# Rotated chunks through ScalarE and a DMA, 512-column passes for paired chunks, and more dummy matmuls at the start

## The chip, the cores and the metric

The kernel runs on one core of one Trainium2 chip. The metric is device time in microseconds, the median of several executions. All times are of that one core; its engines are TensorE (PE, with its weight loads PEld), VectorE (DVE), ScalarE (ACT), GpSimd (POOL) and SyncE (SP), which issues nearly all DMAs.

## The reference

Two layers of a mixer over 256 tokens of width 1024, all in float32. Each layer normalises `x`, projects it to some 9600 columns, runs four causal attentions side by side (A: MoBA, which at 256 tokens is one causal block; B: a three-branch attention with compressed, selected and window keys; C: stick-breaking; D: three dilated window attentions, merged by their softmax denominators), gates each, projects each up to 1024 columns, merges the four with sigmoids, and adds an output projection to `x`. A last norm follows.

```python
def _rope(x, pos):                       # queries and keys of A and D, queries of B, some keys of B
    x1, x2 = x[..., :half], x[..., half:]
    return jnp.concatenate([x1 * cos - x2 * sin, x1 * sin + x2 * cos], axis=-1)
...
h = _rmsnorm(x, norm_w)
proj = jnp.einsum('bsd,dc->bsc', h, w_in)
...                                      # o_a, o_b, o_c, o_d: the four attentions
widened = jnp.stack([_merge_heads(o_a) * jax.nn.silu(ga), ...], axis=2)
u = jnp.einsum('bsiw,iwd->bsid', widened, w_up)
y = jnp.sum(merge_g * u, axis=2)
return x + y @ w_out
```

## The kernel before

**Products in three parts.** Every large product is made from 4-byte operands split into a high and a low half: the weight tile `raw` (512 KB, 128 x 1024) is loaded by SP, ScalarE casts it to the high half `wh` (`emit_hi`, line 327), VectorE subtracts to get the low half `wl` (`emit_lo`, line 335), which also frees `raw` for the next load (`emit_loads`, line 312). The activations are split the same way into `hh` and `hl`. TensorE adds `high x high`, `high x low` and `low x high`. There are 5 buffers for `raw` and 6 for each half. A "half" in the code is one such weight tile.

**Items.** `layer_items` (line 36) is the order of one layer: first `N2` (`av`, `cv`, the values of A and C, tokens as stationary operand, 256 columns of weights moving), then `T` items (weights stationary, the 256 tokens moving) for queries, keys and gates, `K` and `N` items for other values, `W1` for the small network of B, then 16 pairs of `M` (merge gate) and `U` (up projection), and last the output projection: `o0`, `o1` and the pair `o2`, `o3`, 256 columns each. A T item takes two weight tiles and 48 matmuls. `mm_N2` (line 521) picks its passes by which operands are ready; `mm_o0` (line 579) leaves the last quarter of `y` for the end.

**An order written ahead.** The program is built by a planner: `Clock` (line 57) estimates for each engine when it is free and for each tile when it is written, and the builder emits instructions in the order that this clock gives (`run_splits`, `fill`). On the chip each engine then follows its own list strictly in order, and so does SP's list of DMAs.

**PSUM.** Products go to a ring `pp` of 3 banks of 512 columns. What comes after an item is a generator in `POST` (line 1166); it returns the bank with `pp.put`.

**Rotated chunks.** For `aq`, `ak`, `bq` and the six `dq`, `dk` of a layer, `post_rope` (line 675) multiplies the bank by sines, 32 rows at a time and written 32 rows up or down, multiplies it by cosines, frees the bank, lets GpSimd add the two, and then, once a buffer is free, `stack` (line 661) splits the result for the scores:

```python
for r in range(4):
    i, o = slice(32 * r, 32 * r + 32), slice(32 * (r ^ 1), 32 * (r ^ 1) + 32)
    vec.tensor_tensor(out=t2[o], in0=b2[i], in1=sinF[i]..., op=ALU.mult)
vec.tensor_tensor(out=q..., in0=b2, in1=cosF..., op=ALU.mult)
pp.put(bank)
nc.gpsimd.tensor_tensor(out=q, in0=q, in1=t, op=ALU.add)
```

`q` is a buffer of the ring `qkv`, to which four slices of `xt` are lent while `x` is not needed; so these rows read `xt` in some chunks and `qkv` in others, and `t` is `rope`.

**Output.** `post_out` (line 1123) adds a 256-column bank to `x` and squares the new columns for the next norm; `out_done` (line 1245) starts the norm of a token tile `tt` (128 tokens) when its last chunk is done. In the next layer's first item, `norm_T` (line 484) transposes the normed tile on PE. Ahead of the last slot of `o2`/`o3` the tile `tt` = 0 is transposed (line 1330).

**Start.** Four dummy matmuls on a zero tile `warm` (line 1273), eight transposes that spread the norm weight, then the norm of `x` in pieces, its transposes, and the first projection.

Matmuls and vector operations are all recorded on line 151, in the wrapper that keeps the planner's clock; tiles tell them apart.

## Time and profile before

| | us |
|---|---|
| median of 3 executions | 634.83 (634.63 to 635.2) |
| the profiled execution | 634.86 |
| its span, first to last instruction | 632.9 |
| PE busy | 612.2 |
| DVE busy | 482.1 |
| ACT busy | 369.5 |
| POOL busy | 46.3 |

The profile is of one execution. A row "out<-in" names what an instruction writes and reads, with buffer numbers left out. Busy time of PE counts a matmul from its start to a modelled end, so matmuls that follow each other overlap; the distance of their starts is what a matmul costs in a row of them. Idle time carries the name of what ended it. Only idle time on the chain that sets the end costs anything.

### The profile page before, as it was taken

The page shows a single profiled execution, that of the slowest core. Times are in us where ns is not written, and L with a number is a line of the kernel's source. Part 1 is how long each engine was busy: PE and PEld are TensorE (multiplying, and loading weights), DVE is VectorE, ACT ScalarE, POOL GpSimd, SP SyncE. Part 2 cuts the span into 40 slices and gives each one's busy share as a digit, 9 for nine tenths or more (in the row PEclk, how much of TensorE's full clock was granted, in tenths as well). Part 3 has the DMA queues.
Part 4 walks back from the last instruction along what each step waited for, and adds up shares of the span by engine and source line. Part 5 has one row for each costly group of instructions (what it writes and reads, how often), then busy time and mean ns, then how long its engine had stood idle before and what let it go on. Part 6 is the DMA issues. An engine that isn't in the chain of part 4 may idle for free.

```text
span 632.9 us, 12881 instructions
## 1 busy us (share of the span) xinstructions
PE 612.2 (97%) x5192; PEld 587.3 (93%) x5192; DVE 482.1 (76%) x850; ACT 369.5 (58%) x657; POOL 46.3 (7%) x59
## 2 busy tenths in 40 slices
PE   7999999999999999999999999999989999999996
PEld 6999999999998999999999899889989989999995
DVE  5887788999976665677688678899999666566673
ACT  5636744655557888445474564543575678864452
POOL 3020100111200000000001101021110000000000
PEclk9999999999999999999999999999999999999998
DMA  8942456644444345677666155645437344466811
GB/s 282 335 147 79 155 192 243 238 162 148 142 161 153 127 140 168 214 246 237 210 211 227 43 192 167 234 168 208 158 100 223 112 166 150 136 205 193 291 62 67
DMA packets 34907, 112.22 MB, mean 177 GB/s; under 512 B 4256, under 2 KB 5280, under 8 KB 34848
## 3 DMA queue, kind: packets, MB, share of 16 engines
q1 hardware_dynamic: 34560, 111.07, 52.2%
q8 instruction: 41, 0.67, 0.4%
q0 software_dynamic: 144, 0.33, 0.3%
q14 instruction: 18, 0.15, 0.1%
q10 hardware_dynamic: 144, 0.00, 0.0%
HBM read 109.61 MB, written 2.10 MB: 177 GB/s over the span
## 4 chain that ended last, share of the span: by engine, by line
PE 64%; DVE 20%; ACT 7%; issue 6%; DMA 2%; POOL 1%; SPq 0%; POOLq 0%; ACTq 0%; DVEq 0%
PE pp L151 55%; DVE wl L151 8%; DVE rope L151 4%; PE psO L151 3%; PE psT L151 3%; ACT p L151 3%; PE psS L151 3%; ACT wh L151 2%; DVE xt L151 2%; DMA raw<-w_half_dram 2%; DVE hl L151 1%; DVE p L151 1%; DVE pd L151 1%; DVE qkv L151 1%; ACT hh L151 1%
## 5 line engine op out<-in xcount | busy, mean ns | idle before, releaser
L151 PE MATMUL pp<-hh,wh 128*128 128x256 f32 x1008 | 288.2, 286 | 2.2 <-DVE xt L151 1.8
L151 PE MATMUL pp<-hh,wl 128*128 128x256 f32 x1008 | 282.1, 280 | 4.5 <-DVE wl L151 4.4
L151 PE MATMUL pp<-hl,wh 128*128 128x256 f32 x1008 | 280.9, 279 | 0.0
L151 DVE TENSOR_TENSOR wl<-raw,wh 128x1024 fp32r<-128x1024 f32 (+2 forms) x198 | 233.1, 1196 | 48.0 <-ACT wh L151 47.2
L151 ACT CAST wh<-raw 128x1024 fp32r<-128x1024 f32 (+2 forms) x198 | 189.2, 979 | 53.7 <-DMA raw<-w_half_dram 24.3
L151 PEld LDWEIGHTS pp<-hh,wh 128*128 128x128 f32 x1008 | 189.4, 188 | 9.0 <-issue 5.5
L151 PEld LDWEIGHTS pp<-hh,wl 128*128 128x128 f32 x1008 | 189.5, 188 | 6.2 <-DVE wl L151 6.1
L151 PEld LDWEIGHTS pp<-hl,wh 128*128 128x128 f32 x1008 | 189.4, 188 | 0.1
L151 PE MATMUL pp<-wh,hh 128*128 128x256 f32 (+1 forms) x320 | 84.9, 285 | 1.0 <-ACT hh L151 1.0
L151 PE MATMUL pp<-wl,hh 128*128 128x256 f32 (+1 forms) x320 | 83.1, 279 | 1.3 <-DVE wl L151 1.2
L151 PE MATMUL pp<-wh,hl 128*128 128x256 f32 (+1 forms) x320 | 83.4, 281 | 0.0
L151 PEld LDWEIGHTS pp<-wh,hh 128*128 128x128 f32 x320 | 58.3, 192 | 2.5 <-ACT hh L151 1.7
L151 PEld LDWEIGHTS pp<-wl,hh 128*128 128x128 f32 x320 | 57.3, 188 | 1.9 <-DVE wl L151 1.9
L151 PEld LDWEIGHTS pp<-wh,hl 128*128 128x128 f32 x320 | 58.0, 191 | 0.0
L151 ACT ACTIVATE p<-p,small 128x128 f32<-128x128 f32 x96 | 40.0, 449 | 27.8 <-DVE small L151 27.1
L151 DVE TENSOR_TENSOR rope<-pp,sinF 32x512 f32<-32x512 f32 x72 | 49.5, 687 | 3.3 <-PE pp L151 1.4
L151 POOL TENSOR_TENSOR xt<-xt,rope 128x512 f32<-128x512 f32 x14 | 28.0, 1998 | 168.8 <-DVE xt L151 93.2
L151 PE MATMUL pp<-widl,wh 128*128 128x256 f32 x128 | 35.9, 281 | 1.1 <-DVE widl L151 1.1
L151 PE MATMUL pp<-widh,wh 128*128 128x256 f32 x128 | 36.0, 282 | 0.0
L151 PE MATMUL pp<-widh,wl 128*128 128x256 f32 x128 | 35.8, 279 | 0.0
L151 ACT ACTIVATE tm<-pp 128x512 f32<-128x512 f32 x32 | 18.9, 591 | 22.1 <-PE pp L151 22.1
L151 ACT COPY ptr<-psT 128x384 f32<-128x384 f32 x47 | 21.4, 478 | 17.6 <-PE psT L151 17.5
(142 smaller groups left out, 666.6 us busy)
## 6 DMA issues: line engine op xcount, KB each, us to landing
raw<-w_half_dram SPq DMA_DIRECT2D x178, 512.0 KB, 4.2
raw<-w_up_dram SPq DMA_DIRECT2D x32, 256.0 KB, 3.2
raw<-w_kvb_dram SPq DMA_DIRECT2D x4, 536.0 KB, 4.5
xt<-x_in_dram SPq DMA_DIRECT2D x4, 256.0 KB, 3.5
xt<-x_in_dram SPq DMA_DIRECT2D x2, 512.0 KB, 7.1
pd<-norm_w_dram SPq DMA_DIRECT2D x2, 512.0 KB, 5.6
x_mem<-xt SPq DMA_DIRECT2D x2, 512.0 KB, 5.4
xt<-x_mem SPq DMA_DIRECT2D x2, 512.0 KB, 6.0
```

The costliest lines, as they stand in the source:

```text
L151: return f(*a, **k)
```

## The change

- **Rotation.** `post_rope` copies the bank to SBUF on ScalarE and frees it. Four DMAs (`swap_rows`, 64 KB each) write the copy into `rope` with the 32-row groups exchanged. When the planner's clock says that they have landed, VectorE multiplies the exchanged tile by the sines and the copy by the cosines, 128 rows each, and adds the two. The sign table is stored in the other order. For `bq` the copy is also the unrotated query, as before.
- **Paired chunks.** `av`/`cv` and now also `o0`/`o1` and `o2`/`o3` are computed as 512 columns at once: a weight tile holds 2 of the 8 row blocks of both chunks, a bank holds one token tile of both. In the last layer's last token tile, `o2`/`o3` stay two banks of 256 columns. `o0`/`o1` do the first three weight tiles for both token tiles, then the fourth. `av`/`cv` are copied out in four pieces by ScalarE or VectorE (`post_copy2`). Planned positions follow.
- **Dummies.** 7 more dummy matmuls after the spread of the norm weight, 2 after the first transposes of the norm and 5 after the second. They are not entered in the planner's clock.

```diff
             it.append(("U", (i, c), 1))
-    it += [("N", "o0", 2), ("N", "o1", 2), ("N2", ("o2", "o3"), 4)]
...
         d = {"U": 1.3, "W1": 0.6}.get(kind, 2.6)
+        if kind == "N2":
+            pos += [p_ + 1.3 * j for j in range(n)]
+            p_ += 4 * d
+            continue
         for j in range(n):
             pos.append(p_)
-            if not (kind in ("N", "N2", "K") and j % 2 == 0):
-                p_ += d if kind not in ("N", "N2", "K") else 2 * d
+            if not (kind in ("N", "K") and j % 2 == 0):
+                p_ += d if kind not in ("N", "K") else 2 * d
...
+        left = [6] * 4
         count = [0, 0]
-        todo = [(tt, j, kk, p) for tt in range(2) for j in range(2) for kk in range(4) for p in range(3)]
+        todo = [(tt, j, p) for tt in range(2) for j in range(4) for p in range(3)]
...
             for i in range(2):
-                k = 2 * kk + i
-                c = count[j]
-                count[j] += 1
-                mm(banks[j][:, 256 * tt:256 * tt + 256], x[0][:, i, :], x[1][:, 256 * (k % 4):256 * (k % 4) + 256],
-                   start=(c == 0), stop=(c == 47))
-            h = 2 * j + kk // 2
-            left[h] -= 1
-            if not left[h]:
-                release(h0 + h)
+                c = count[tt]
+                count[tt] += 1
+                mm(banks[tt], x[0][:, i, :], x[1][:, 512 * i:512 * i + 512], start=(c == 0), stop=(c == 23))
+            left[j] -= 1
+            if not left[j]:
+                release(h0 + j)
             n += 1
-            if n % 3 == 0:
+            if n % 2 == 0:
                 yield
         yield
...
-    def mm_o0(banks, h0):
-
...
+    def mm_o(bank, tt, h0, j, c0, c1):
+
+        for i in range(2):
+            k = 2 * j + i
+            hi, lo = (w[h0 + j][:, 512 * i + c0:512 * i + c1] for w in (his, los))
+            a, b = (y[1][:, k, 128 * tt:128 * tt + 128] for y in (hh, hl))
+            o = bank[:, 0:c1 - c0]
+            mm(o, a, hi, start=(k == 0), stop=False)
+            mm(o, a, lo, start=False, stop=False)
+            mm(o, b, hi, start=False, stop=(k == KT - 1))
+            yield
...
+    def swap_rows(out_, in_):
+
+        for r in range(4):
+            dma(out=out_[32 * (r ^ 1):32 * (r ^ 1) + 32], in_=in_[32 * r:32 * r + 32])
+        clk.t["dma"] = max(clk.t["dma"], clk.idle(out_), clk.ready(in_)) + 0.7
+        clk.wr.setdefault(out_.name, {})[(0, 128, 0, 512)] = clk.t["dma"] + 2.0
+        clk.rd.setdefault(in_.name, {})[(0, 128, 0, 512)] = clk.t["dma"] + 2.0
+
     def post_rope(l, name, bank):
-        q, t = take(qkv), rope.get()
+        c, t = take(qkv), rope.get()
+        nc.scalar.copy(c, bank)
+        pp.put(bank)
+        swap_rows(t, c)
+        yield when(t)
+        q = c
         if name == "bq":
-            T_[l, "bqr"] = r = take(qkv)
-            nc.scalar.copy(r, bank)
-        b2 = bank.rearrange("p (a t) -> p a t", a=2)
-        t2 = t.rearrange("p (a t) -> p a t", a=2)
-        for r in range(4):
-            i, o = slice(32 * r, 32 * r + 32), slice(32 * (r ^ 1), 32 * (r ^ 1) + 32)
-            vec.tensor_tensor(out=t2[o], in0=b2[i], in1=sinF[i].unsqueeze(1).to_broadcast([32, 2, S]), op=ALU.mult)
-        vec.tensor_tensor(out=q.rearrange("p (a t) -> p a t", a=2), in0=b2,
-                          in1=cosF.unsqueeze(1).to_broadcast([128, 2, S]), op=ALU.mult)
-        pp.put(bank)
-        nc.gpsimd.tensor_tensor(out=q, in0=q, in1=t, op=ALU.add)
+            T_[l, "bqr"] = c
+            q = take(qkv)
+        v = lambda x: x.rearrange("p (a t) -> p a t", a=2)
+        rows = lambda x: x.unsqueeze(1).to_broadcast([128, 2, S])
+        vec.tensor_tensor(out=v(t), in0=v(t), in1=rows(sinF), op=ALU.mult)
+        vec.tensor_tensor(out=v(q), in0=v(c), in1=rows(cosF), op=ALU.mult)
+        vec.tensor_tensor(out=q, in0=q, in1=t, op=ALU.add)
         rope.put(t)
...
+    def post_copy2(l, names, banks):
+
+        for j, name in enumerate(names):
+            T_[l, name] = take(qkv)
+        for tt in range(2):
+            for j, name in enumerate(names):
+                copy_to(T_[l, name][:, 256 * tt:256 * tt + 256], banks[tt][:, 256 * j:256 * j + 256])
+            pp.put(banks[tt])
+        done.update((l, name) for name in names)
...
-    def post_out(l, c, tt, bank):
-        xs = xt[:, tt, 256 * c:256 * c + 256]
-        vec.scalar_tensor_tensor(out=xs, in0=bank[:, 0:256], scalar=0.25, in1=xs, op0=ALU.mult, op1=ALU.add)
+    def post_out(l, c, n, tt, bank):
+
+        c0, c1 = 256 * c, 256 * (c + n)
+        xs = xt[:, tt, c0:c1]
+        vec.scalar_tensor_tensor(out=xs, in0=bank[:, 0:c1 - c0], scalar=0.25, in1=xs, op0=ALU.mult, op1=ALU.add)
         pp.put(bank)
-        square(tt, 256 * c, 256 * c + 256, c)
...
-        if kind == "N2" and name[0] == "o2":
+        if kind == "N2" and name[0] == "o0":
+
+            banks = [pp.get(), pp.get()]
+            for js in ((0, 1, 2), (3,)):
+                for tt in range(2):
+                    for j in js:
+                        yield (lambda: mm_o(banks[tt], tt, h0, j, 0, 512),
+                               (lambda: out_done(l, 0, 2, tt, banks[tt])) if j == 3 else None, [h0 + j] if tt else [], j, tt)
+        elif kind == "N2" and name[0] == "o2":
             for tt in range(2):
-                for j in range(2):
+                last = l == L - 1 and tt
+                for c0, c1 in ((0, 256), (256, 512)) if last else ((0, 512),):
                     bank = pp.get()
-                    yield (lambda: mm_N(bank[:, 0:256], tt, h0 + 2 * j, 256, hh[1], hl[1]),
-                           lambda: out_done(l, 2 + j, tt, bank), [h0 + 2 * j, h0 + 2 * j + 1] if tt else [])
+                    for j in range(4):
+                        yield (lambda: mm_o(bank, tt, h0, j, c0, c1),
+                               (lambda: out_done(l, 2 + c0 // 256, (c1 - c0) // 256, tt, bank)) if j == 3 else None,
+                               [h0 + j] if tt and c1 == 512 else [], j, tt)
         elif kind == "N2":
             banks = [pp.get(), pp.get()]
-            yield (lambda: mm_N2(banks, h0, pend.pop(1), l),
-                   lambda: [add_post(post_copy(l, name[j], banks[j])) for j in range(2)], [])
...
+            yield (lambda: mm_N2(banks, h0, pend.pop(1), l), lambda: add_post(post_copy2(l, name, banks)), [])
...
-        p1.put(warm)
+        def keep_warm(n):
+            for _ in range(n):
+                tc.nc.tensor.matmul(psO[:, 0, 0:128], warm[:, 0:128], warm[:, 0:128], start=True, stop=True)
+
+        keep_warm(7)
...
         norm_T(0, 0, xs[0][0], 0)
+        keep_warm(2)
...
         norm_T(0, 1, xs[0][1], 0)
+        keep_warm(5)
+        p1.put(warm)
...
-                if kind == "N2" and name[0] == "o2" and si == 3 and l + 1 < L:
+            for si, (work, after, freed, *part) in enumerate(gen):
+
+                if kind == "N2" and name[0] == "o2" and si == 6 and l + 1 < L:
                     norm_b(0, pend.pop(0), l + 1)
...
-                first = pos[lo_] + (2.6 if kind in ("N", "K") and si else 0.0)
+                first = pos[lo_] + (2.6 if kind in ("N", "K") and si else 5.2 if kind == "N2" and tt else 0.0)
...
+    def n2_type(w):
+        w = w.reshape(KT, 128, 512).transpose(1, 0, 2)
+        return [w[:, 2 * j:2 * j + 2].reshape(128, -1) for j in range(4)]
...
-    rt = np.concatenate([cos, cos, sin, -sin], 1).T.reshape(2, 64, S)
+    rt = np.concatenate([cos, cos, -sin, sin], 1).T.reshape(2, 64, S)
```

## Rows read from the trace of the kernel before

**Rows 1.** The page's busy table: busy us, share of the span, instructions.
```profile
PE 612.2 (97%) x5192; PEld 587.3 (93%) x5192; DVE 482.1 (76%) x850; ACT 369.5 (58%) x657; POOL 46.3 (7%) x59
```

**Rows 2.** The page's chain that ended last, by engine.
```profile
PE 64%; DVE 20%; ACT 7%; issue 6%; DMA 2%; POOL 1%; SPq 0%; POOLq 0%; ACTq 0%; DVEq 0%
```

**Rows 3.** Table by stretches: length, busy us per engine, clock, DMA.
```profile
core 0: us, PE busy (x) PEld busy (x) DVE busy (x) ACT busy (x) POOL busy (x), PEclk, DMA share, GB/s
10.00:20.00 10.00, 9.80 (x66) 9.81 (x67) 9.56 (x12) 6.01 (x9) 2.27 (x6) 1.00 0.98 292
...
130.00:166.00 36.00, 33.47 (x284) 32.65 (x283) 34.79 (x61) 19.06 (x33) 7.69 (x5) 1.00 0.42 132
...
430.00:475.00 45.00, 41.86 (x346) 40.46 (x345) 41.72 (x76) 23.42 (x38) 7.79 (x5) 1.00 0.44 153
```

**Rows 4.** Waits (us, times, longest): whole span, last row 300 to 345 us.
```profile
PE pp L151 <- DVE wl L151: 5.6, 8, 1.6
PE pp L151 <- DVE xt L151: 1.8, 2, 0.9
...
PEld psT L151 <- DVE qkv L151: 0.5, 2, 0.2
```

**Rows 5.** Timeline of PE: start, us, instruction, idle before it and releaser.
```profile
42.25 0.35 PE L151 MATMUL pp<-hh,wh 128*128 128x256 f32 x1 [0.91 <-DVE xt L151]
...
163.56 0.28 PE L151 MATMUL pp<-hl,wh 128*128 128x256 f32 x1
165.11 0.39 PE L151 MATMUL pp<-hh,wl 128*128 128x256 f32 x1 [1.27 <-DVE wl L151]
```

**Rows 6.** Groups by shape: count, busy us, mean ns, idle before.
```profile
L151 DVE TENSOR_TENSOR rope<-pp,sinF 32x512 f32<-32x512 f32 x72 | 49.5, 687 | 3.3 <-PE pp L151 1.4 <-ACT qkv L151 0.8
L151 POOL TENSOR_TENSOR xt<-xt,rope 128x512 f32<-128x512 f32 x14 | 28.0, 1998 | 168.8 <-DVE xt L151 93.2 <-ACT wh L151 41.1 <-DMA raw<-w_half_dram 21.3
L151 DVE TENSOR_TENSOR qkv<-qkv,tm 128x512 f32<-128x512 f32 x24 | 16.6, 692 | 0.8
L151 DVE TENSOR_TENSOR xt<-pp,cosF 128x512 f32<-128x512 f32 x14 | 9.7, 692 | 0.2
L151 DVE SCALAR_TENSOR_TENSOR xt<-pp,xt 128x256 f32<-128x256 f32 x16 | 6.7, 421 | 6.2 <-PE pp L151 6.2
L151 ACT COPY xt<-pp 128x512 f32<-128x512 f32 x8 | 4.6, 584 | 0.6 <-PE pp L151 0.5
```

**Rows 7.** Chain in order of time: start, us, what.
```profile
176.00 3.53 PE pp L151 x30
...
605.89 14.17 PE pp L151 x125
```

**Rows 8.** Timeline of PE, the 512-column scores of one head.
```profile
184.08 0.63 PE L151 MATMUL psS<-hl,hh 128*128 128x512 f32 x2
184.55 0.28 PE L151 MATMUL pp<-widh,wh 128*128 128x256 f32 x1
```

**Rows 9.** Chain in order of time, the start.
```profile
10.20 2.07 PE pp L151 x8
...
13.12 1.28 PE pp L151 x6
...
15.20 16.87 PE pp L151 x149
```

**Rows 10.** Timeline, the first microseconds: SP's issues and PE's dummies.
```profile
0.74 1.81 SPq L1266 DMA_DIRECT2D xt<-x_in_dram  x4
...
1.49 2.08 PE L151 MATMUL psO<-p 128*128 128x128 f32 x8 [1.49 <-DVE p L151]
```

**Rows 11.** DMA issues: count, KB each, median us to landing.
```profile
raw<-w_half_dram SPq DMA_DIRECT2D x178, 512.0 KB, 4.2
...
out_dram<-qkv SPq DMA_DIRECT2D x4, 256.0 KB, 2.6
...
w2k<-w2k_in_dram SPq DMA_DIRECT2D x2, 128.0 KB, 5.3
```

More of the change, by code (lines that the diff above doesn't have):

```diff
@@ L521, in mm_N2, with operands @@
     def mm_N2(banks, h0, pend, l):
-        left = {h: 12 for h in range(4)}
+        left = [6] * 4
         count = [0, 0]
-        todo = [(tt, j, kk, p) for tt in range(2) for j in range(2) for kk in range(4) for p in range(3)]
+        todo = [(tt, j, p) for tt in range(2) for j in range(4) for p in range(3)]
         waits = [(1, j) for j in range(2)]
-        def operands(tt, j, kk, p):
-            h = h0 + 2 * j + kk // 2
-            if h not in los or (tt, kk // 2) in waits:
+        def operands(tt, j, p):
+            h = h0 + j
+            if h not in los or (tt, j // 2) in waits:
                 return None
-            a = (hh, hh, hl)[p][0][:, 2 * kk:2 * kk + 2, 128 * tt:128 * tt + 128]
+            a = (hh, hh, hl)[p][0][:, 2 * j:2 * j + 2, 128 * tt:128 * tt + 128]
             return a, (his, los, his)[p][h]
@@ L1130, in post_out @@
                 fin[tt] = [qkv.get(), qkv.get()]
-            vec.tensor_tensor(out=fin[tt][c // 2][:, 256 * (c % 2):256 * (c % 2) + 256], in0=xs,
-                              in1=nws[L][:, 256 * c:256 * c + 256], op=ALU.mult)
+            o = c0 % 512
+            vec.tensor_tensor(out=fin[tt][c // 2][:, o:o + c1 - c0], in0=xs, in1=nws[L][:, c0:c1], op=ALU.mult)
     fin = {}
@@ L1243, with out_done @@
     pend = {}
-    def out_done(l, c, tt, bank):
-        post_out(l, c, tt, bank)
-        if c == 3:
+    def out_done(l, c, n, tt, bank):
+        post_out(l, c, n, tt, bank)
+        if c + n == 4:
             if l + 1 < L:
@@ L1294 @@
         weighted(0, 0)
-        square(0, 512, 1024, 1)
+        square(0, 512, 1024, 2)
         norm_rstd(0)
@@ L1298 @@
         square(1, 0, 512, 0)
-        square(1, 512, 1024, 1)
+        square(1, 512, 1024, 2)
         scaled(0, 0, "v")
@@ L1327 @@
             gen = slots_of(l, kind, name, h0)
-            for si, (work, after, freed) in enumerate(gen):
-                if kind == "N2" and name[0] == "o2" and si == 3 and l + 1 < L:
+            for si, (work, after, freed, *part) in enumerate(gen):
+                if kind == "N2" and name[0] == "o2" and si == 6 and l + 1 < L:
                     norm_b(0, pend.pop(0), l + 1)
@@ L1333 @@
                     lo_, hi_ = h0 + si, h0 + si + 1
-                elif kind == "N2" and name[0] == "av":
-                    lo_, hi_ = h0, h0 + 1
                 elif kind == "N2":
-                    lo_, hi_ = h0 + 2 * (si % 2), h0 + 2 * (si % 2) + 2
+                    j, tt = part or (0, 0)
+                    lo_, hi_ = h0 + j, h0 + j + 1
                 else:
@@ L1349 @@
                     ins = [hl[0]]
-                else:
-                    tt = si // 2 if kind == "N2" else si
-                    ins = [hl[1 if name[0][0] == "o" else 0][:, :, 128 * tt:128 * tt + 128]]
+                elif kind == "N2" and part:
+                    ins = [hl[1][:, 2 * j:2 * j + 2, 128 * tt:128 * tt + 128]]
+                else:
+                    tt = 0 if kind == "N2" else si
+                    ins = [hl[0][:, :, 128 * tt:128 * tt + 128]]
                 run_splits(HORIZON)
@@ L1405, in t_type @@
         return [w[:, :, 128 * j:128 * j + 128].reshape(128, -1) for j in range(w.shape[2] // 128)]
+    def n2_type(w):
+        w = w.reshape(KT, 128, 512).transpose(1, 0, 2)
+        return [w[:, 2 * j:2 * j + 2].reshape(128, -1) for j in range(4)]
     for l in range(L):
         for kind, name, n in layer_items():
-            for nm in (name if kind == "N2" else (name,)):
-                if kind in ("N", "N2") and nm[0] == "o":
-                    c = int(nm[1])
-                    half += n_type(w_out[l][:, 256 * c:256 * c + 256])
-                elif kind in ("N", "N2"):
+            if kind == "N2":
+                if name[0][0] == "o":
+                    c = 256 * int(name[0][1])
+                    half += n2_type(w_out[l][:, c:c + 512])
+                else:
+                    half += n2_type(np.concatenate([w_in[l][:, cols[nm]:cols[nm] + 256] for nm in name], axis=1))
+            for nm in () if kind == "N2" else (name,):
+                if kind == "N":
                     half += n_type(w_in[l][:, cols[nm]:cols[nm] + 256])
```

25 lines of the change are left out of this document (5 added, 20 removed).

## The prediction, made before the result

> **What bounds the kernel now.** I read the page's busy table first: TensorE is busy 612.2 us of 632.9 [rows 1], so no change can gain much more than the 20.7 us in which it idles, unless its own work shrinks. Part of those lie before the first projection and behind the last matmul. The chain of work that ended last runs through PE for 64% and through VectorE for 20% [rows 2]: in some stretches VectorE sets the pace. The table by stretches says where: from 130 to 166 us DVE is busy 34.79 of 36 us while PE idles 2.53, and from 430 to 475 us 41.72 of 45 while PE idles 3.14 [rows 3]. These are the two layers' rotated chunks of the dilated attention (`dq`, `dk`). The waits name what is late: PE waits 8 times for a low half `wl`, which VectorE makes, 5.6 us in all, and twice, 1.8 us, for `xt`, the last VectorE product of a rotation that still holds a PSUM bank [rows 4]. In the timeline the longest of the first layer is the gap from 163.56 to 165.11, and the bank shows at 42.25 [rows 5]. A matmul's end is drawn 0.28 us after its start, but its successor normally starts after 0.117 (below), so each of the 10 stalls costs 0.16 more than the idle shown: 7.4 + 10 x 0.16 = 9.0 us.
>
> **The rotation, moved.** A rotated chunk costs VectorE four products of 32 rows (0.687 each) and one of 128 rows (0.692), 3.44 us, and GpSimd an add of 2.0 us [rows 6]. After: one ScalarE copy out of PSUM (0.584), four DMAs that exchange the 32-row groups, then two products and the add on VectorE, all in SBUF; `qkv<-qkv,tm` is the same operation on the same shape at 0.692, so 2.08 us [rows 6]. VectorE saves 1.36 us a chunk; 72 / 4 = 18 chunks make 24.6 us, 16.4 of it on the 12 dilated chunks. ScalarE gains 16 copies (`bq` had one), 9.3 us, and has room: it is busy 19.06 of 36 and 23.42 of 45 us in the stretches of [rows 3]. The bank comes free after the copy, 0.6 us, and not after 3.4. Those two stretches hold 4 + 4 chunks, so 10.9 us of VectorE time goes where PE loses about 7: enough to lift all stalls if nothing new is late. I do not take all 9.0. PE that runs on meets the next late operand earlier (DVE would still be some 85% busy), and the exchange adds a wait. I take two thirds, **-6.0 us**, with bounds of -9 and 0; what is worse than 0 is the second rival.
>
> The exchange's queues: SP issues the four DMAs in its order, behind weight loads that wait for a free `raw` buffer and ahead of later ones. What waits behind them waits for a ScalarE copy at most. A DMA costs SP 1.81 / 4 = 0.45 us to issue [rows 10], so 1.8 us a chunk on a queue that mostly stands waiting.
>
> **512 columns.** `av`/`cv` and the four output chunks are 288 passes of 256 columns in a layer; they become 144 of 512, except 24 that stay in halves in the last stage: 264 long passes in all. What does a long one cost? In the output projection a 256-column pass now takes 14.17 / 125 = 113.4 ns; elsewhere 3.53 / 30 = 117.7 is common [rows 7]. The only 512-column matmuls of the trace, in the scores of branch b, start at 184.08 and the next work at 184.55: 0.47 / 2 = 235 ns [rows 8]. Two short passes of 113.4 are 226.8. By that row a long pass is no cheaper, it costs 8 ns more. I take 233, a little under the row because it stands in a stretch of the slower pace: 264 x 6.2 = **+1.6 us**, with bounds of 0 (226.8, the better pace kept) and +2.2 (235). The Trainium skill ("TensorE: Matmul & The Clock Gate", Back-to-back issue gap) gives N / 2.4 + 2.5 ns for a lone warm matmul, 216 ns for 512 columns; by it the sum would have -2.9 us here and not +1.6. This case's row at 235 speaks against it for these 4-byte operands.
>
> One more wait comes with the wide output pass. Between the layers the transposes of the next norm already wait 0.5 us for `qkv` [rows 4]. Now both chunks of a token tile end together, so the update of `x` ahead of it is 512 wide (0.69 for 0.421 [rows 6]) and so is the square: **+0.5 us**, bounds 0 and +1, once. The tail behind the last matmul stays, since that stage keeps its halves.
>
> **Dummy matmuls.** The first projection starts at 10.20. Its first 8 passes take 2.07 us and the 6 behind 13.12 1.28 us (213 ns), against 16.87 / 149 = 113.2 from 15.20 on [rows 9]: 256 columns in 213 ns is TensorE's 1.2 GHz level, in 113 it is 2.4; the granted-clock column shows nothing below 1.00 here, so I go by the starts. Until 10.2 PE had worked in pieces with gaps of about a microsecond; from 10.2 it worked unbroken and was fast 5 us later. The dummies close those gaps, so I expect it fast by about 9 us. At full pace these 14 passes would save 14 x 0.1 = 1.4 us, and the 8 transposes between them up to 1 more; but DVE, which makes the operands, is busy 9.56 of the 10 us from 10 to 20 [rows 3], so I take **-1.3 us**, bounds -2.4 and +2. The bad bound: a dummy is two records of 2.08 / 8 = 0.26 us [rows 10] at the slow level, the transposes and the first projection stand behind 7, 2 and 5 of them in PE's order, and 14 x 0.52 = 7.3 us is more than PE has free before 10.2: if the clock did not rise, the first projection would come some 4 us late, of which the fast clock behind it gives back about 2.
>
> Copies of `av`/`cv` (halves instead of whole banks) and the weight order cost some tenths of a microsecond that lie beside PE's work; if that cover went they would still be under 0.5 us.
>
> **Sum.** 634.86 (the profiled run; its span is 632.9, with 2.0 around it, and the median of three is 634.83, the same) - 6.0 + 1.6 + 0.5 - 1.3 = **629.7 us**.
>
> **Rivals.**
> - *Long passes are cheaper.* 113.4 ns is 6.7 above 256 columns at 2.4 GHz (106.7). If that is a fixed cost of a pass, a long one takes 213.3 + 6.7 = 220 ns: 264 x -6.8 = -1.8 us in place of +1.6, so 626.3 us. Against: 235 ns [rows 8]. Chance 0.2. The formula of the skill page named above is of this kind; by its 216 ns the time would be 625.2.
> - *The exchange lands late: slower.* DVE works in order; where the scheduler places the product before the data has landed, it stands, and the `wl` splits that PE needs stand behind it. The code allows 0.7 + 2.0 + 0.2 = 2.9 us after the copy. Issuing four takes 1.8 us, and the nearest DMAs land 2.6 us (`out`, quiet), 4.2 (`raw`) and 5.3 us (`w2k`, loaded) after issue [rows 11]: 4.4 to 7.1. The shortfall of 1.5 to 4.2 us per chunk must first eat the 1.36 saved and DVE's idle time in these stretches, (1.21 + 3.28) / 8 = 0.56 a chunk [rows 3]; it decides from 1.9 us on. At 2.9 us, 12 dilated chunks lose 12 x 1.0 = 12 us: 634.9 + 12 + 0.8 = 647.7; at 2.2 us it is 639.3. For it: SP's queue is in order and shared with the loads. Against: DVE already lags the plan where it is the bound, and a lag covers a late landing. The Trainium skill ("SBUF — State Buffer", Door 1) says that a transfer over 32 partitions reaches 8 of 16 ports and that two do not add up; by that page's 27.2 GB/s a port I estimate 1.2 us for the 256 KB of a chunk, and the shortfall would be 0.6 larger. No row here shows it. Chance 0.13.
> - *The stalls only move.* PE gains nothing in the rotated stretches because attention or `wh` on ScalarE, which now also copies, is late next: 634.86 + 1.6 + 0.5 - 1.3 = 635.7, no change. Against: ScalarE's share there is about half. Chance 0.1.
>
> **How the numbers follow.** Forecast 0.57, rivals 0.2, 0.13 and 0.1. The forecast's own range is 624 to 634. The 80% range takes in the cheap long passes with the full -9 (622) and reaches into the mild end of the late exchange (637). A measurement of this kernel can tell about 0.2% (1.3 us) from no change. Faster: the forecast and the first rival, with a little of the former at the edge: 0.77 + 0.02 = 0.79; same 0.08 (most of the third rival); slower 0.13.
>
> **What would show it.** Right: DVE's total falls from 482 to about 458 us and POOL's to about 10; the `wl` waits of PE shrink by more than half; no wait for `xt` at a bank behind the first `K` item; starts of 512-column passes 226 to 236 ns apart; 256 columns in 113 ns by 12 us. Wrong: long waits of DVE for `rope` from a DMA with `wl` behind them (second rival), 220 ns or less between long passes (first), a first projection later than 11 us, or ScalarE's `wh` in place of `wl` in the waits (third).

## The result and the profile after

| | us |
|---|---|
| kernel before, beside it, median of 5 executions | 634.83 |
| changed kernel, median of 5 (629.18 to 632.28) | 629.46 |
| ratio of the means, 95% interval | 0.9927 (0.9899 to 0.9956) |
| the profiled execution of the changed kernel | 632.28, its span 630.2 |

The change makes the kernel 0.7% faster; forecast were 629.7 us. The five executions lie in two groups, three at 629.2 to 629.5 and two at 631.7 and 632.3; the profile is of the upper group, and the experiment `a_again` gives one of the lower, with a span of 627.4. Both are used below.

First the page: busy time by engine and the chain that ended last, to be read beside [rows 1, 2].

```profile
PE 614.3 (97%) x4956; PEld 580.6 (92%) x4956; DVE 441.3 (70%) x803; ACT 378.0 (60%) x664; POOL 9.9 (2%) x41
...
PE 84%; DVE 5%; ACT 4%; DMA 4%; issue 3%; SPq 0%; POOLq 0%; POOL 0%; ACTq 0%; DVEq 0%
```

VectorE's part of the chain fell from 20 to 5%, and its total by 40.8 us, not by the 24.6 of the forecast. The stretch from 130 to 166 us, one of the two in [rows 3], in the table by stretches:

```profile
130.00:166.00 36.00, 36.00 (x309) 35.76 (x308) 28.89 (x65) 21.15 (x36) 0.00 (x0) 1.00 0.61 196
```

TensorE is busy 36.00 of 36 us where it was 33.47, VectorE 28.89 where it was 34.79. The waits of the changed kernel (engine and tile, what it waited for: us in all, times, longest):

```profile
PE pp L151 <- ACT sg L151: 3.3, 2, 2.3
PE pp L151 <- DVE widl L151: 2.0, 2, 1.4
PE psO L151 <- DVE p L151: 1.5, 1, 1.5
PE pp L151 <- DVE wl L151: 1.0, 3, 0.5
...
DVE wl L151 <- ACT wh L151: 64.8, 64, 3.0
...
DVE rope L151 <- DMA rope<-xt: 11.7, 6, 3.9
```

TensorE's 5.6 us for `wl` in [rows 4] are 1.0 now, and the wait for `xt` at a bank is gone. Two are new: TensorE waits 3.3 us for `sg`, the last thing that ScalarE makes of a bank of the `K` item (once in each layer), and VectorE waits 11.7 us for exchanged rows.

Where the time went, by stage. Each border is the start of a stage's first matmul in the timeline of PE: the first `T` item, the first merge item, the first output pass, and the same in the second layer; "first" counts from the start of the span, "output 2" to the end of the last matmul.

| us | first `av`/`cv` ends | rotated 1 | merges 1 | output 1 and next `av`/`cv` | rotated 2 | merges 2 | output 2 |
|---|---|---|---|---|---|---|---|
| before | 24.35 | 136.27 | 135.41 | 35.19 | 137.47 | 136.01 | 21.93 |
| changed, profiled first | 24.08 | 135.91 | 135.74 | 36.73 | 134.25 | 134.78 | 22.41 |
| changed, `a_again` | 24.29 | 133.17 | 135.81 | 36.74 | 134.20 | 134.47 | 22.41 |
| rotation alone | 24.67 | 134.47 | 135.41 | 36.20 | 133.08 | 137.00 | 22.73 |
| 512 columns alone | 24.08 | 138.18 | 136.20 | 36.73 | 138.16 | 136.20 | 22.41 |
| dummies alone | 23.35 | 138.00 | 135.25 | 35.19 | 137.66 | 136.02 | 21.93 |

For `a_again` against before: the rotated stretches give 3.10 + 3.27 = 6.4 us, the output stages cost 1.55 + 0.48 = 2.0, the merges give 1.1, the start nothing. In sum 5.5, the difference of the two spans. The border between "rotated" and "merges" does not part the rotation from the rest: the last rotated chunks are worked on behind it, and the two longest of the stops that the prediction counted, at 165.11 and 473.96 us, lie in the merges. So the rotation's gain is to be read from both together, 7.5 us. In the profile of the rotation alone the granted clock was 0.95 nearly throughout, in the others of the table 1.00, so its row is not quite on a par with them.

### The profile page after: what moved, and what is told of

It is laid out like the page before. It is cut to its first block, busy times and chain, and to the rows that moved or that the text cites. A ratio compares the mean times of both kernels' runs of the same rounds, so it can differ in the third digit from the quotient of the medians.

```text
span 630.2 us, 12473 instructions
## 1 busy us (share of the span) xinstructions
PE 614.3 (97%) x4956; PEld 580.6 (92%) x4956; DVE 441.3 (70%) x803; ACT 378.0 (60%) x664; POOL 9.9 (2%) x41
## 4 chain that ended last, share of the span: by engine, by line
PE 84%; DVE 5%; ACT 4%; DMA 4%; issue 3%; SPq 0%; POOLq 0%; POOL 0%; ACTq 0%; DVEq 0%
PE pp L151 72%; PE psS L151 4%; PE psO L151 4%; PE psT L151 3%; DMA raw<-w_half_dram 2%; ACT p L151 2%; DVE wl L151 2%; DMA raw<-w_kvb_dram 1%; ACT wh L151 1%; DVE p L151 1%; ACT hh L151 1%; DMA rope<-xt 1%; DVE qkv L151 1%; DVE xt L151 0%; DVE small L151 0%
## 5 line engine op out<-in xcount | busy, mean ns | idle before, releaser
L151 DVE TENSOR_TENSOR wl<-raw,wh 128x1024 fp32r<-128x1024 f32 (+2 forms) x198 | 221.5, 1136 | 65.5 <-ACT wh L151 64.8
L151 PE MATMUL pp<-wh,hh 128*128 128x256 f32 (+2 forms) x232 | 72.9, 327 | 0.2 <-ACT hh L151 0.2
L151 PE MATMUL pp<-wl,hh 128*128 128x256 f32 (+2 forms) x232 | 72.4, 324 | 0.5 <-DVE wl L151 0.5
L151 PE MATMUL pp<-wh,hl 128*128 128x256 f32 (+2 forms) x232 | 71.9, 324 | 0.0
L151 ACT ACTIVATE p<-p,small 128x128 f32<-128x128 f32 x96 | 40.2, 451 | 24.1 <-DVE small L151 23.3
L151 PEld LDWEIGHTS pp<-wh,hh 128*128 128x128 f32 x232 | 43.4, 188 | 5.2 <-issue 0.8
L151 PEld LDWEIGHTS pp<-wl,hh 128*128 128x128 f32 x232 | 43.4, 188 | 4.6 <-DVE wl L151 0.7
L151 PEld LDWEIGHTS pp<-wh,hl 128*128 128x128 f32 x232 | 43.7, 188 | 4.1
L151 ACT ACTIVATE tm<-pp 128x512 f32<-128x512 f32 x32 | 19.0, 594 | 24.6 <-PE pp L151 24.5
L151 ACT COPY ptr<-psT 128x384 f32<-128x384 f32 x50 | 22.7, 478 | 14.7 <-PE psT L151 14.4
L151 ACT COPY xt<-pp 128x512 f32<-128x512 f32 (+2 forms) x29 | 14.1, 501 | 28.4 <-PE pp L151 17.2
L151 DVE RECIPROCAL small<-small 128x2 f32<-128x2 f32 (+1 forms) x34 | 5.7, 168 | 31.7 <-ACT p L151 21.2
```

What stands on the lines that cost most here:

```text
L151: return f(*a, **k)
```

## The experiments

Medians are set against the kernel before as it ran beside each of the three sets of experiments (634.96, 634.31 and 635.05 us); intervals are those of the ratio. These three differ by 0.7 us, so a difference between kernels of two sets can be off by as much.

**One part at a time.** The first three kernels are the kernel before with one part of the diff each; the fourth is the changed kernel again.

`e_rope` takes `swap_rows`, `post_rope` and the sign table:

```diff
+        nc.scalar.copy(c, bank)
+        pp.put(bank)
+        swap_rows(t, c)
+        yield when(t)
```

`e_wide` takes `mm_N2`, `mm_o`, `post_copy2`, `post_out` and the planned positions:

```diff
-    it += [("N", "o0", 2), ("N", "o1", 2), ("N2", ("o2", "o3"), 4)]
+    it += [("N2", ("o0", "o1"), 4), ("N2", ("o2", "o3"), 4)]
```

`e_dummy` takes the 14 dummies:

```diff
+        keep_warm(7)
...
+        keep_warm(2)
...
+        keep_warm(5)
```

> The kernel before with the rotation alone moved to a ScalarE copy, four DMAs and three VectorE operations; passes of 256 columns and the start stay. If the forecast's step is right, this alone gives about -6.0 us (627 to 631 us), TensorE's waits for wl shrink by more than half, and VectorE's total falls from 482 us to 458 or less. If the stalls only move (third rival), it is within 1 us of the kernel before. If the exchange lands too late (second rival), VectorE waits for rope before its products and the time rises above 636. The trace of the changed kernel shows VectorE waiting 11.7 us in all for rope and a new stop of TensorE of about 2.5 us near 44 us, where the third bank of the ring is held; if that stop belongs to the rotation and not to the wide passes, it is here too, near the same place, and the gain is 3 to 5 us and not 6.

> The kernel before with the 512-column passes alone (av/cv and the four output chunks); rotation and start stay. By the forecast +1.6 us for 264 passes at 233 ns and +0.5 for the norm between the layers: about +2.1 us, 636 to 638. By the first rival (220 ns) -1.3 us, about 633.5. The traces of before and after show 233 ns between long passes, so the first rival should fall; what is open is whether the wide passes cost more than +2.1 us elsewhere, for instance because the 256-column passes behind them run at 118 ns where they ran at 113: that would show as a slower pace of the T items right behind the first item, and give +3 to +5 us.

> The kernel before with the 14 dummy matmuls alone. The forecast says -1.3 us (first projection no later than 10.2 us, 256 columns in 113 ns by 12 us instead of 15). The rival by the trace of the changed kernel: VectorE, which makes hl and wl, is the bound from 10 to 15 us, TensorE then waits for it, and the gain is 0.3 us or nothing. Bad end: dummies at the slow level push the first projection back, +2 us.

> The changed kernel once more, for a second profile beside the same runs. Its executions so far lie at 629.2 to 629.5 or at 631.7 to 632.3 us, and the profiled one was of the upper group: there TensorE stood 2.5 us at 44 us and its 256-column passes were 167 ns apart for the next 4 us at a granted clock of 0.50 to 0.95. Theory: the two groups differ by that clock drop; a profile of an execution near 629.3 shows the stop at 44 us with a granted clock of 1.00 behind it and passes 118 ns apart. Rival: the stop itself is shorter in the faster ones, since the exchange lands earlier there; then VectorE's wait for rope ahead of it is under 2 us and not 3.5.

| kernel | us, median | against before | ratio, 95% |
|---|---|---|---|
| `e_rope` | 628.75 | -6.2 | 0.9909 (0.9890 to 0.9927) |
| `e_wide` | 640.21 | +5.3 | 1.0085 (1.0072 to 1.0098) |
| `e_dummy` | 634.02 | -0.9 | 0.9990 (0.9982 to 0.9999) |
| `a_again` | 629.13 | -5.8 | 0.9911 (0.9899 to 0.9924) |

The rotation brings what the forecast said, although the stop at the `K` item's bank, with which 3 to 5 us were expected, is there too (1.33 us up to 45.95, in the first layer alone). Of VectorE's 40.8 us it accounts for 39.5 (442.6 us busy). The dummies bring something, near the lower end of what can be told. The 512-column passes cost 5.3 us, not 2.1, and the three single effects add up to -1.9 where together they give -5.8. The table by stage says where the wide passes lose the rest: 1.9 us in the first rotated stretch, 0.7 in the second and 1.0 in the merges. The waits of `e_wide`:

```profile
PE pp L151 <- DVE wl L151: 6.6, 11, 1.6
PE pp L151 <- DVE xt L151: 1.9, 2, 1.2
PE psT L151 <- DVE qkv L151: 1.6, 2, 1.2
```

TensorE has more stops (11 for `wl`, where there were 8); in the four rotated and merge stages its idle time grows from 10.4 to 11.9 us. That is 1.5 of the 3.6 us. The wide passes need not be the reason for it: `e_dummy`, which has none, idles 11.9 us there too in its profile (635.66 us, its slowest execution). About as much, 1.5 us, is what the expectation named, a slower pace of the short passes: in these stages 560 of them start 115 ns or less ahead of the next matmul, in the kernel before 876, and those up to 130 ns apart add up to 14.5 and 13.0 us over 113 ns each. Theory A is that the stops come where VectorE still sets the pace, and that the rotation in SBUF removes them too, so that it is worth more beside the wide passes than alone; theory B looks to the pace of the passes. The second run of experiments tests both.

The profile of `a_again` bears out the theory on the two groups only in part. These are the stretches from 44 to 52 us, first of the profile of 632.28 us, then of `a_again` (length, busy us of PE, PEld, DVE, ACT, POOL, granted clock, DMA):

```profile
44.00:46.00 2.00, 0.33 (x3) 0.12 (x2) 1.97 (x5) 0.00 (x0) 0.00 (x0) 1.00 0.13 51
46.00:48.00 2.00, 1.38 (x11) 1.38 (x12) 1.58 (x6) 1.12 (x5) 0.00 (x0) 0.95 0.00 0
48.00:50.00 2.00, 2.00 (x11) 2.00 (x11) 0.00 (x0) 2.00 (x3) 0.00 (x0) 0.50 0.01 4
50.00:52.00 2.00, 2.00 (x14) 2.00 (x14) 1.81 (x4) 1.93 (x4) 0.40 (x2) 0.70 0.00 0
```

```profile
44.00:46.00 2.00, 1.25 (x11) 1.05 (x10) 1.83 (x7) 0.48 (x3) 0.00 (x0) 1.00 0.00 0
46.00:48.00 2.00, 2.00 (x20) 2.00 (x19) 0.42 (x2) 1.98 (x4) 0.00 (x0) 1.00 0.01 4
48.00:50.00 2.00, 2.00 (x19) 2.00 (x19) 1.17 (x2) 1.95 (x4) 0.00 (x0) 1.00 0.00 0
```

In `a_again` the clock stays at 1.00 and 19 matmuls start in 2 us instead of 11; but the stop ahead of it is shorter too, 1.02 us from start to start instead of 2.57. So the rival was right on the stop and the theory on the clock: a long stop comes with a fall to the 1.2 GHz level behind it. How the long stop comes about is in the timelines of the slower execution, of SP, VectorE, ScalarE and TensorE (start, us, instruction, idle before it and releaser):

```profile
36.20 2.89 SPq L677 DMA_DIRECT2D rope<-xt  x4
...
43.65 0.69 DVE L151 TENSOR_TENSOR rope<-rope,sinF 128x512 f32<-128x512 f32 x1 [0.47 <-DMA rope<-xt]
...
45.58 0.28 DVE L151 TENSOR_TENSOR rope<-pp,cosT 128x128 f32<-128x128 f32 x1
...
46.38 0.19 ACT L151 ACTIVATE sg<-pp 128x12 f32<-128x12 f32 x1
...
46.62 0.39 PE L151 MATMUL pp<-hh,wh 128*128 128x256 f32 x1 [2.29 <-ACT sg L151]
```

SP issues the exchange of `aq` behind two weight loads, and VectorE, which takes the rows in its order, has to wait for them until 43.65 (until 42.31 in `a_again`). Only behind the three operations on them comes the rotation of the `K` item, at 45.58, and behind that the ScalarE work that frees its first bank; TensorE needs this bank at 44.2 and gets it at 46.6. (The expectations speak of it as the third bank.)

**What the wide passes cost, what the landing costs, and the pace of short passes.** `x_nowide` is `e_rope` with the dummies. `x_split` cuts each long pass of the changed kernel in two, in place. `x_land4` allows 4.0 us for the landing. `x_flip` adds three transposes.

`x_split`, and in the same way in `mm_o`:

```diff
-                mm(banks[tt], x[0][:, i, :], x[1][:, 512 * i:512 * i + 512], start=(c == 0), stop=(c == 23))
+                for e in (0, 256):
+                    mm(banks[tt][:, e:e + 256], x[0][:, i, :], x[1][:, 512 * i + e:512 * i + e + 256],
+                       start=(c == 0 and e == 0), stop=(c == 23 and e == 256))
```

`x_land4`, which also waits for a free `rope` buffer:

```diff
-        clk.wr.setdefault(out_.name, {})[(0, 128, 0, 512)] = clk.t["dma"] + 2.0
+        clk.wr.setdefault(out_.name, {})[(0, 128, 0, 512)] = clk.t["dma"] + 4.0
...
-        c, t = take(qkv), rope.get()
+        c, t = take(qkv), take(rope)
```

`x_flip`:

```diff
+                if kind == "M" and name == (ORDER[2], 1) and si == 0:
+                    b = rot(psT)
+                    for k in range(3):
+                        nc.tensor.transpose(b[:, 128 * k:128 * k + 128], iden, iden)
```

> Rotation and dummies moved as in the changed kernel, passes of 256 columns as before. Alone the parts measured -6.2 (rotation), +5.3 (512 columns) and -0.9 us (dummies), in sum -1.9; together they give -5.8. So two parts interact by 4 us. Theory A: the 512-column passes cost 3 us more than their 2.2 only where VectorE sets the pace; with the rotation moved they cost about 2, so this kernel gives 627 (629.1 - 2.1). Theory B: with the rotation moved the 256-column passes run at 118 ns almost everywhere (as the profile of the rotation alone shows, 269 passes at 113 to 115 ns instead of 1554), two of them cost 235 and a long pass at 233 costs nothing; then this is 628 to 629. If the wide passes always cost 5.3: 623.9. If they are a gain: above 629.5.

> The changed kernel with each 512-column pass made as two passes of 256 columns on the same weights, in the same place and order; nothing else differs. If two short passes run at 113.4 ns, 264 x 6.2 = 1.6 us less: 627.5. If they run at the slower pace of 118, 264 x 235.5 against 233: 0.6 us more, 629.8. By the first rival (a fixed cost per pass that a long one pays once) 264 x 6.7 = 1.8 us more, 630.9.

> The changed kernel with the planner allowing 4.0 instead of 2.0 us for the landing of the exchanged rows (and waiting for a free rope buffer where it found one before), so that VectorE reaches the products later and other work goes ahead of them. If the late landing is what is left of the second rival, VectorE's waits for rope (9.1 us in 6) fall below 3 us, TensorE's stops at 45 us (0.9) and 351 us (1.2) vanish, and the time is 1 to 2.5 us lower, 626.6 to 628. Rival: those stops come from the third bank and an in-order VectorE whatever the allowance; then it stays within 0.7 us of 629.1, or is longer because the scores start later.

> The changed kernel with one group of three extra 128-column transposes of the identity into a transposes' bank in each layer, ahead of the tenth of the 16 merge and up items. In all traces the 256-column passes run at one of two paces, 113 or 118 ns, which stay until other matmuls come between; from the tenth item on 462 passes run at 118 in the changed kernel. If the pace is set anew by such a group, as it was at 530.0 us of the second profile (45 passes at 113 behind three transposes, 118 again behind five more), 2 x 462 x 4.6 ns = 4.3 us less, less 2 x 0.35 us for the groups: 625.5; with one layer of two 628. If the pace belongs to the stretch and not to what went ahead, 0.7 us more: 629.8.

| kernel | us, median | ratio to before, 95% |
|---|---|---|
| `x_nowide` | 630.0 (626.45 to 632.36) | 0.9923 (0.9898 to 0.9949) |
| `x_split` | 627.76 | 0.9896 (0.9883 to 0.9909) |
| `x_land4` | 637.74 | 1.0056 (1.0043 to 1.0069) |
| `x_flip` | 630.92 | 0.9942 (0.9930 to 0.9954) |

`x_split` against `a_again`: two short passes in place of a long one give 1.4 us by the medians, with overlapping intervals, and 0.7 when each is set against the kernel before beside it; 1.6 were expected at the pace of 113 ns. The stages tell it better: the two output stages, with 216 of the 264 long passes, take 35.90 and 21.93 us for 36.74 and 22.41, so 1.3 us less, 6.1 ns a long pass.

`x_nowide` could not decide between theories A and B, since its executions scatter over 6 us. The scatter goes with the granted clock: 626.45 and 627.24 us at a mean clock of 0.999 and 0.998, 629.61 to 632.36 at 0.996 to 0.992. Its profile, at 629.61, has a stop from 43.31 to 45.79 at the same bank of the `K` item, and a clock of 0.59 and 0.56 in the 4 us behind. At the undisturbed 626.45 to 627.24 it lies 1.9 to 2.7 us below `a_again`, as theory A has it. The premise of theory B falls as well: the profile of `e_rope` ran at a granted clock of 0.95, and there even the output passes, which start 113 ns apart in every other kernel that has them short, start 118 ns apart; so its few fast passes can't be put down to the rotation.

The hope behind `x_land4` fails. VectorE no longer waits for `rope` at all, as expected, but the stops at that bank stay (45.35 to 46.68 and 353.82 to 355.15), so it is not VectorE's standing alone that makes them, but that the bank's work comes behind the exchange in its order. The late products cost more elsewhere: the merges take 138.57 and 138.60 us for 135.81 and 134.47, with TensorE waiting 9 times for `wl` and not 3, four of them in the merges and 0.8 to 0.9 us each. Why `wl` is late there, some 55 to 65 us behind the last exchange, I did not trace; ScalarE, busy 42.1 of the 50 us from 200 to 250 (40.4 in `a_again`), carries more.

```profile
PE pp L151 <- DVE wl L151: 4.8, 9, 0.9
PE pp L151 <- DVE widl L151: 2.2, 2, 1.1
PE pp L151 <- ACT sg L151: 2.1, 2, 1.1
```

That of `x_flip` fails as well. Behind the three transposes the passes of the first layer go on 117 to 119 ns apart; 22 at 113 follow only behind transposes of the kernel's own, at 242.0, and then the stretch is back at 118. In the second layer four passes at 113 follow the group, and then 118 again. The two merge stages take 1.8 us more than in `a_again`. The pace was not set for the stretch this way; but since the kernel's own transposes came six passes behind each group, the trial says little about what sets it:

```profile
240.13 0.55 PE L151 MATMUL psT<-iden 128*128 128x128 f32 x3 [0.32 <-DVE ptr L151]
240.43 0.36 PE L151 MATMUL pp<-hh,wh 128*128 128x256 f32 x1
240.63 0.28 PE L151 MATMUL pp<-hl,wh 128*128 128x256 f32 x1
240.75 0.28 PE L151 MATMUL pp<-hh,wl 128*128 128x256 f32 x1
```

**The `K` item's banks freed, and the exchange doubled.** In the `y` kernels ScalarE copies each bank of the `K` item out behind its token tile, and the rotation of the keys reads the copy, for which it also waits for a free `rope` buffer; on the changed kernel, on `x_split` and on `x_nowide`.

```diff
+    def bkv_out(l, tt, bank):
+        if not tt:
+            T_[l, "kvc"] = take(qkv)
+        nc.scalar.copy(T_[l, "kvc"][:, 256 * tt:256 * tt + 256], bank[:, 0:256])
+        act(out=sg[:, tt, :], in_=bank[:, 256:268], func=AF.Tanh, scale=0.5)
+        pp.put(bank)
...
-            t1, t2 = ropes(banks[tt][:, 0:128], 2, (tt,))
+            t1, t2 = ropes(c[:, 256 * tt:256 * tt + 128], 2, (tt,))
```

`x_twice`, on the changed kernel:

```diff
-        for r in range(4):
+        for r in list(range(4)) * 2:
```

> The changed kernel with the two banks of the K item copied out by ScalarE right behind each token tile (256 columns, and the gate's tanh), so that they come free before VectorE has rotated the keys; the rotation then reads the copy. Theory: what is left of the late exchange is that the third bank is held, because VectorE, in order, waits for the exchanged rows of aq and then rotates the K item; if so, TensorE's stops near 45 us (0.9 to 2.5) and 351 us (1.2) vanish and with them the fall of the granted clock behind the longer of them: 626.5 to 627.5, and no group of executions near 632. Rival: the next late thing (casts of hh for the keys on ScalarE, then wl) stops TensorE a few us later: within 0.7 us of 629.1.

> Both at once: passes of 256 columns (627.8 alone) and the K item's banks freed by a copy. If the two add, 625.5 to 626.3, below every kernel so far.

> Rotation and dummies on the kernel before, without 512-column passes, and with the K item's banks freed by a copy. Without the copy this kernel had executions from 626.5 to 632.4 us: TensorE stopped 2.5 us at 43 us and its granted clock fell to 0.56 to 0.59 for the next 4 us in the profile. If the stop brings the fall, and the bank brings the stop, all executions lie at 625.5 to 627 now. If the spread comes from elsewhere it stays.

> The changed kernel with the four exchange DMAs of each chunk issued twice (the second four write the same rows again), so that the rows land some 2.4 us later and SP is busy longer, while VectorE's order and the planner's allowance stay. By the price of the second rival a further 2.4 us against a slack of about 1.9 us for each dilated chunk costs 12 x 0.5 to 1.0 = 6 to 12 us, and VectorE waits 25 us or more for rope. If VectorE's lag covers it, under 2 us more than 629.1, with the loss at the third bank near 45 and 351 us alone. A loss of 2 to 6 us would say that the slack is larger than the prediction took.

| kernel | us, median | ratio to before, 95% |
|---|---|---|
| `y_kbank` | 625.88 (625.18 to 626.03) | 0.9850 (0.9837 to 0.9863) |
| `y_split_kbank` | 623.95 | 0.9823 (0.9810 to 0.9837) |
| `y_nowide_kbank` | 623.0 (622.31 to 623.51) | 0.9808 (0.9795 to 0.9821) |
| `x_twice` | 670.84 | 1.0550 (1.0527 to 1.0574) |

All three `y` kernels came out below what was expected. The bank is shown: freeing it gives 3.3 us on the changed kernel, its second group of executions is gone, and the scatter of `x_nowide` shrinks from 6 us to 1.2. No profile of a `y` kernel has more than 0.25 us of idle time at that bank. Not all of the 3.3 us is the bank: TensorE's idle time in the four rotated and merge stages falls from 4.5 us in `a_again` to 2.2, and the rest goes with the pace, 684 fast passes for 413. The kernels of this set also price the wide passes without the long stop: 625.88 - 623.95 = 1.9 us for the width of the passes alone, 625.88 - 623.0 = 2.9 for the whole part. That is not the 5.3 of `e_wide`, as theory A has it, though nearer 3 than 2, and not the nothing of theory B; that VectorE's stops make the difference is in part argued, since the pace changed as well. The best kernel of the study is the rotation and the dummies without the wide passes, with the bank freed: 1.9% below the kernel before. Its busy table and its waits:

```profile
PE 609.1 (98%) x5220; PEld 588.4 (95%) x5220; DVE 445.0 (72%) x817; ACT 378.2 (61%) x674; POOL 10.0 (2%) x41
```

```profile
PE psO L151 <- DVE p L151: 1.5, 1, 1.5
PE pp L151 <- DVE widl L151: 0.9, 1, 0.9
PE pp L151 <- DVE wl L151: 0.7, 3, 0.3
```

`x_twice` is the dose for the second rival, and it was larger than meant. Its waits, and SP's timeline at the first chunk:

```profile
PE pp L151 <- ACT sg L151: 13.2, 2, 7.3
PE pp L151 <- DVE wl L151: 12.4, 10, 4.2
...
DVE rope L151 <- DMA rope<-xt: 41.8, 13, 5.7
...
ACT wh L151 <- DMA raw<-w_half_dram: 45.3, 19, 6.1
```

```profile
31.07 7.85 SPq L677 DMA_DIRECT2D rope<-xt  x8
```

Eight DMAs take SP 6 to 8 us, mostly over 7, where four mostly take 2.4, since the second four wait until the first have landed (32.7 us of SP's time in all); so the rows come some 5 us later, not 2.4, and SP's loads behind them too: ScalarE waits 45.3 us for `raw`, in `a_again` 26.3. The time rises by 41.7 us, where 6 to 12 were expected. By the second rival's own price, 12 chunks x (5.0 - 1.9) = 37 us. That is near, but two causes are in it, the late rows and the late loads, and no run parts them. Its stops of 2.4 us and more are followed by the low clock as well; one of them, from 165.48 to 167.93:

```profile
167.00:169.00 2.00, 1.07 (x9) 1.07 (x10) 2.00 (x3) 1.95 (x5) 0.00 (x0) 0.98 0.16 20
169.00:171.00 2.00, 2.00 (x12) 2.00 (x11) 1.97 (x4) 1.39 (x2) 0.00 (x0) 0.50 0.95 299
```

## Why the prediction came out right, point by point

- **What bounds the kernel.** Right. Where VectorE's load fell, TensorE's idle time went with it: none is left from 130 to 166 us, where it was 2.53 [rows 3].
- **The rotation, -6.0.** Right alone, -6.2; in `a_again` 7.5 us, in the rotated and merge stages together. But "two thirds of 9.0" stood in part for the wrong reason. PE did not simply meet the next late operand; the 1.5 us that `a_again` lacks of the 9.0 are less than what one new stop in each layer costs (1.02 and 1.33 us from start to start), at the `K` item's banks, where the bank wait of [rows 5] at 42.25 came back in another form. With the bank freed, the step brings more than the bound of -9: `e_dummy` against `y_nowide_kbank`, the same but for the rotation and the bank, is 634.02 against 623.0. The bound counted the waits for `wl` and `xt` alone, 7.4 of the 10.4 us that TensorE idles in the rotated and merge stages; in `y_nowide_kbank` 2.0 us are left there.
- **VectorE's saving, 24.6 us.** Mis-sized: 40.8. The counted operations are right; 11.5 us more come from the splits: 162 of `wl` take 195.8 us instead of 205.2, and 32 half ones 22.0 instead of 24.1, because GpSimd's adds no longer hold them up (last section). The trace of the kernel before had this already. The last 4.7 I have not traced.
- **Long passes at 233 ns.** Right, in the changed kernel's first output stage:

```profile
295.74 0.39 PE L151 MATMUL pp<-wh,hh 128*128 128x512 f32 x1
295.97 0.39 PE L151 MATMUL pp<-wl,hh 128*128 128x512 f32 x1
296.20 0.39 PE L151 MATMUL pp<-wh,hl 128*128 128x512 f32 x1
```

  The +1.6 measured 1.4 (`x_split`) and 1.9 (the `y` pair), with 6.1 ns a pass in the output stages for 6.2. The first rival (220 ns) is out, and with it the 216 ns of the Trainium skill ("TensorE: Matmul & The Clock Gate", Back-to-back issue gap), with which this trace doesn't agree: 233 for these 4-byte operands.
- **The norm between the layers, +0.5.** Right, as near as it can be told: with short passes in the same places (`x_split`) that stage takes 35.90 us, 0.71 more than before.
- **What this part lacked.** The sum assumed that the parts don't meet. On the kernel before, the wide passes cost 2.4 us more (5.3 against 2.9) than with the rotation moved and the bank freed. Had they been forecast alone, at +2.1, the forecast would have been wrong.
- **The dummies, -1.3.** Mis-sized. Alone -0.9; beside the wide passes nothing: `av`/`cv` ends at 24.29 in `a_again` and at 24.08 in `e_wide`, which has no dummies. The chain of `a_again` says why:

```profile
10.04 0.69 DVE hl L151
10.73 0.67 DVE qkv L151 x2
...
11.68 0.47 DVE qkv L151
12.14 0.31 DVE hl L151
...
12.66 1.22 DVE wl L151
...
13.93 12.18 PE pp L151 x58
```

  From 10 to 13.9 us it runs through VectorE, and TensorE starts its long unbroken row at 13.93; in `e_wide` that is 13.70. A faster TensorE arrived earlier at the same operands. The forecast named VectorE as the reason to take less, and took too little off. That PE would be fast early was right: ten dummy records ahead of the first projection take 1.28 us in `a_again`, where eight took 2.08 [rows 10].
- **The second rival.** It did not decide, but it happened in small: 11.7 us of VectorE's waiting for rows (9.1 in `a_again`), and up to 3.3 us of the end time, most of it at one place that the prediction did not name. Its terms held: four DMAs take SP 2.4 us where 1.8 were taken, and the rows land 2.0 to 6.7 us after issue, 4.0 in the middle. It looked for the loss at the `wl` splits behind the waiting product; it was at a PSUM bank behind it.
- **The third rival.** Right in one row: `sg` from ScalarE in place of `xt` from VectorE.
- **What would show it.** `wl` waits down by more than half: yes, 5.6 to 1.0. No wait for `xt` at a bank behind the first `K` item: yes by name, no in substance. Starts 226 to 236 ns apart: yes. POOL to about 10: yes, 9.9. DVE to about 458: no, 441.3. 256 columns in 113 ns by 12 us: not to be seen in the changed kernel, whose passes are long there; in `y_nowide_kbank`, where they are short, yes, from 10.94 us on.

That the sum met the time is partly luck: the dummies, which were to give 1.3 us, gave nothing in `a_again`, and the rotation, with the merges that come behind it, gave 1.5 us more than was taken. Two errors nearly cancel. Nor did the forecast set anything for the pace of the short passes, which in the rotated and merge stages of `a_again` cost 2.5 us more than before (15.6 us over 113 ns each, where it was 13.0).

## What to carry to other kernels

When work of a stalling engine is sent by way of a DMA, look beyond that engine's next task: in an in-order queue the work behind the late product may hold a PSUM bank, and the ring's next user pays. Free such banks by a copy ahead of anything that waits for a landing; here that was worth some 3 us, about half of what the rotation brought, while a larger allowance in the plan cost some 9. Ask also what the other engine's work does to the engine that is the bound: more than a quarter of VectorE's relief here came from GpSimd's adds going away. And measure the parts of a change alone as well as together: a part that costs 3 us beside the others can cost 5 without them.

## What the runs showed of the hardware that I had not expected

- **Two paces of the same pass.** 256-column passes start either 113 or 118 ns apart, for tens to hundreds of passes on end, at a granted clock of 1.00. Counted over the passes into `pp`, from a pass's start to the next matmul's, 1386 of 4272 took 115 or less in the kernel before, 413 of 3744 in `a_again`, 1302 of 4272 in `y_nowide_kbank`, and 158 of 4272 in the profile of `e_rope`, at a granted clock of 0.95. (An expectation above has 1554 and 269 for the kernel before and `e_rope`; by this count they are 1386 and 158.) All passes of the kernel before that took 116 to 121 cost 12.1 us over 113. The pace changes where other matmuls come between or the kind of item changes, but not always, and `x_flip` could not set it. Its cause stays open.
- **A stop has an echo.** Stops of 2.4 us and more went with 3 to 4 us at the 1.2 GHz level behind or at their end, in the changed kernel, `x_nowide` and `x_twice` (there 7 us with the three longest, of 4.5 to 7.6); behind the stop of 1.55 us in [rows 5] and the 1.02 of `a_again` the granted clock stayed at 1.00. In the first profile that made a stage 2.7 us longer whose stop was 1.55 longer.
- **GpSimd holds VectorE up.** The same subtraction of two SBUF tiles, in `e_rope` and then in `e_wide`, where GpSimd still adds (count, busy us, mean ns, idle before):

```profile
L151 DVE TENSOR_TENSOR wl<-raw,wh 128x1024 fp32r<-128x1024 f32 x162 | 195.7, 1220 | 60.7 <-ACT wh L151 59.9
```

```profile
L151 DVE TENSOR_TENSOR wl<-raw,wh 128x1024 fp32r<-128x1024 f32 x162 | 206.3, 1288 | 43.8 <-ACT wh L151 43.3
```

  With GpSimd's 36.8 us of adds gone it takes 68 ns less in the mean. In the kernel before, nine of the 162 began while an add ran, and these took 2.30 to 2.32 us; all the others took 1.20 to 1.28. The timelines of VectorE and of GpSimd at one of them, where the second split of the pair starts at 441.20 and ends 1.1 us behind the add:

```profile
440.07 3.44 DVE L151 TENSOR_TENSOR wl<-raw,wh 128x1024 fp32r<-128x1024 f32 x2
...
440.32 2.10 POOL L151 TENSOR_TENSOR xt<-xt,rope 128x512 f32<-128x512 f32 x1 [12.54 <-DVE xt L151]
```

  Each lost 1.09 us, as did two of the half splits: 12.0 us in all, near the 11.5 by busy time. The Trainium skill ("GPSIMD Engine Reference", Specifications) says that GpSimd shares its SBUF interfaces with VectorE and contends with instructions that have two SBUF inputs; this agrees. It was no term of the sum.
